# Keeping the whole TensorE stream in source order in a two-layer mixer kernel

## The chip, the cores and the metric

The kernel runs on one core of one Trainium2 chip. The metric is the device time of the launch in microseconds (us). Two runs of the kernel before gave 1919.79 and 1923.13 us, median 1921.46 us. A separate execution was profiled; its own time is 1923.45 us.

## The reference, cut to what matters

The program computes two layers of a hybrid backbone for 256 context tokens and 256 latent tokens of width 2048. In each layer the tokens are RMS-normed and modulated by a vector that comes out of `c_silu @ ada_w` (adaLN), go through one input projection `h @ w_in`, and are split into four head groups: bidirectional mLSTM, bidirectional retention, softmax attention with rotary positions, and bidirectional gated DeltaNet. Each group's output is multiplied by a SiLU gate, the groups are concatenated, go through `w_out`, are normed again and added to the stream. Layer 1 needs its latent half alone at the output. In short:

```
mod = silu(c) @ ada_w + ada_b
h   = rms_norm(x, pre_w) * (1 + sc) + sh
u   = h @ w_in                       # all four groups' q, k, v, gates
y   = [mlstm(u), retention(u), attention(u), gated_delta(u)]   # each * silu(z)
x   = x + gt * rms_norm(concat(y) @ w_out, post_w)
```

The mLSTM and the DeltaNet need gates: a log-sigmoid and a softplus of a few columns of `u`, then cumulative sums over tokens. The DeltaNet also needs a triangular solve per chunk and a state that is carried from chunk to chunk. All arithmetic is in float32; the large products split each operand into a rounded part and a remainder and add three products.

## The kernel before, in words

**The stream of large products.** A `Run` is one group of output columns of `w_in` or `w_out`. `emit` (L946) walks its contraction in steps of 128 rows (16 steps k), and each step adds three matmuls per output tile into a PSUM tile `acc` (L969), twelve in a step of four tiles. `Stream` (L899) loads a raw weight tile with a DMA on the SP queue (L915), rounds it on ScalarE (`whi`, L926) and takes the remainder on VectorE (`wlo`, L927); there are three `raw` tiles and four `whi` and `wlo` tiles, so splits run at most three steps ahead of the matmuls that use them. `acc` has four buffers. When a run's last two steps are done per output tile, `evac` takes the tile out of PSUM.

**The small work** is written as Python generators, one for each task: the gates (`gate_tiles`, L219), the mLSTM (L333), retention, attention (L499 on), the DeltaNet's solve, its doubling and its chunk recurrence (class `Delta`, `double`, `pair`), column sums, the transposes ahead of layer 1 (`h_half`, L1215) and those ahead of `w_out` (`transposed`, L1484 on). After each step k of the large stream, `emit` calls `pump`, which lets every live task emit its instructions up to its next `yield`. So the source order is: twelve large matmuls, a piece of each task, twelve large matmuls, and so on. `finish` runs a task to its end at one place, with no large matmuls between its pieces. Small PSUM results use a pool `mx` of three buffers.

**What sets the order on an engine.** The framework's scheduler orders each engine's instructions by its own reckoning of when inputs are ready; among ready instructions the one that comes first in the source goes first. [...] One place, the products with `ada_w` of layer 0 (`ada_products`, L1056 on, L1074), sits in a block `manual_schedule` for TensorE, in which the source order holds among the instructions of the block.

Names that the prediction uses: `gps` (L283 to L286) are the matmuls of the gates' cumulative sums, `g_lf` (L264) their last input; in layer 0 they are emitted after the first twelve matmuls of the run `m_k` that follows the gate columns' last evacuation. `a_pq` (L527) transposes softmax weights `a_p` (L520). `d_py` (L721) opens the DeltaNet's doubling, on tiles `d_T` that a DMA brings. `d_pu` (L838), `d_pS` (L851), `d_ks` (L826), `d_po` (L865, L867) are the steps of its recurrence, `d_W` (L804) the decayed scores that free the PSUM tile the second `d_pu` needs. `h_ps` (L1226) transposes the normed rows `yo` (L1186) for layer 1.

Of the kernel before, what the change touches and what calls it, by code (L numbers as in the profile page):

```python
# [70 lines left out]
def setup(ctx, tc, cst):  # L71
    E = Env()
    nc = tc.nc
    E.nc, E.tc = nc, tc
    E.clock = 0
    E.tasks, E.free, E.live = [], list(range(NSLOT)), {}
    E.cp = ctx.enter_context(tc.tile_pool(name="cp", bufs=1))
    E.ly = ctx.enter_context(tc.tile_pool(name="ly", bufs=1))
    E.bp = ctx.enter_context(tc.tile_pool(name="bp", bufs=1))
    E.tp = ctx.enter_context(tc.tile_pool(name="tp", bufs=5))  # L80
    E.sp = ctx.enter_context(tc.tile_pool(name="sp", bufs=1))
    E.wp = ctx.enter_context(tc.tile_pool(name="wp", bufs=4))
    E.hp = ctx.enter_context(tc.tile_pool(name="hp", bufs=8))
    E.acc = ctx.enter_context(tc.tile_pool(name="acc", bufs=4, space=PSUM))
    E.mx = ctx.enter_context(tc.tile_pool(name="mx", bufs=3, space=PSUM))
    E.dr = ctx.enter_context(tc.tile_pool(name="dr", bufs=1, space=DRAM))
    ct = E.ct = E.cp.tile([P, C_END], F32, name="ct")
    nc.scalar.dma_start(out=ct[:, :C_UP], in_=cst[:, :C_UP])
    E.ident = ct[:, C_ID:C_UP]
    E.up = ct[:, C_UP:C_LO]  # L90
    E.lo = ct[:, C_LO:C_COS]
    E.cos = ct[:, C_COS:C_SIN]
    E.sin = ct[:, C_SIN:C_DL]
    E.dl = ct[:, C_DL:C_END]
    E.ones = E.cp.tile([P, P], F32, name="ones")
    nc.gpsimd.memset(E.ones, 1.0)
    E.mhalf = E.cp.tile([P, 16], F32, name="mhalf")
    nc.gpsimd.memset(E.mhalf, -0.5)
    E.xd = E.dr.tile([2, 32 * 129 * P], F32, tag="xd", name="xd")
    return E  # L100
# [1542 lines left out]

@with_exitstack
def hybrid_dit(ctx: ExitStack, tc: tile.TileContext, I):
    nc = tc.nc
    E = setup(ctx, tc, I.cst)
    x_in = [I.ctx[0, 0:P], I.ctx[0, P:2 * P], I.x[0, 0:P], I.x[0, P:2 * P]]
# [172 lines left out]
```

## Time and profile before

| | |
|---|---|
| median of two runs | 1921.46 us |
| profiled execution, its time | 1923.45 us |
| profiled execution, its span | 1921.7 us |
| TensorE busy | 1848.4 us, 96% |
| VectorE busy | 1341.9 us, 70% |
| ScalarE busy | 813.1 us, 42% |
| mean granted TensorE clock | 0.992 |
| bytes moved | 344.84 MB, mean 179 GB/s |

The span is the time from the first to the last instruction; the execution's own time is 1.75 us longer. Busy time is the union of an engine's instruction records. PE is the matmul row of TensorE, PEld its weight loads, DVE is VectorE, ACT is ScalarE, SP the queue that issues DMAs. In the timeline a row may merge several instructions of a kind; the bracket at its end is the engine's idle time before it and what ended it.

### The profile page before, as it was taken

To read this page: it belongs to the slowest core of one execution; us is meant where nothing else is said; L and a number is where in the kernel's file an instruction comes from. 1 tells how busy PE (TensorE), PEld (TensorE's weight loads), DVE (VectorE), ACT (ScalarE), POOL (GpSimd) and SP (SyncE) were. 2 spreads that over 40 slices of the span, in tenths; PEclk is the share of its full clock that TensorE was granted. 3 is DMA by queue.
4 is the path that set the end of the run, shared out by engine and by line. 5 is a ranking of instruction groups with operands and counts; after the bars stand their busy time and mean duration, and the time that the engine had idled before them with its cause. 6 is when DMAs were issued, how large, how long until landed. Compare 5 with 4: busy or idle time off the path is not lost. (4 is left out here: it accounts for less than half of the span.)

```text
span 1921.7 us, 29531 instructions
## 1 busy us (share of the span) xinstructions
PE 1848.4 (96%) x10836; PEld 1527.6 (79%) x10836; DVE 1341.9 (70%) x2714; ACT 813.1 (42%) x1591; POOL 132.1 (7%) x162
## 2 busy tenths in 40 slices
PE   5999999999999999999999999999999999999997
PEld 3677887777878877788888868978988898888886
DVE  3455689999986896889743578347856476849765
ACT  5322333334342434434342456333435354446453
POOL 0000011121000100000000000000002010000000
PEclk8999999999999999999999999999999999999999
DMA  9887545666655649545423576535744255765464
GB/s 290 275 295 239 183 124 160 194 194 199 220 159 153 198 128 273 170 132 169 133 94 103 180 234 219 148 111 175 252 156 153 92 170 148 189 186 162 134 227 157
DMA packets 265294, 344.84 MB, mean 179 GB/s; under 512 B 48266, under 2 KB 142638, under 8 KB 265150
## 3 DMA queue, kind: packets, MB, share of 16 engines
q1 hardware_dynamic: 264416, 342.71, 57.5%
q8 instruction: 85, 1.39, 0.3%
q14 instruction: 59, 0.48, 0.1%
q10 hardware_dynamic: 734, 0.26, 0.1%
HBM read 321.26 MB, written 17.98 MB: 177 GB/s over the span
## 5 line engine op out<-in xcount | busy, mean ns | idle before, releaser
L926 ACT CAST whi<-raw 128x512 fp32r<-128x512 f32 (+2 forms) x736 | 426.6, 584 | 767.0 <-PE acc L969 667.3
L927 DVE TENSOR_TENSOR wlo<-raw,whi 128x512 fp32r<-128x512 f32 (+2 forms) x736 | 474.1, 649 | 346.7 <-ACT whi L926 338.2
L969 PE MATMUL acc<-h_hi,whi 128*128 128x512 f32 (+1 forms) x1088 | 410.5, 378 | 2.4 <-DVE yo L1555 2.4
L969 PE MATMUL acc<-h_hi,wlo 128*128 128x512 f32 (+1 forms) x1088 | 398.7, 368 | 2.9 <-DVE wlo L927 2.9
L969 PE MATMUL acc<-h_lo,whi 128*128 128x512 f32 (+1 forms) x1088 | 399.9, 368 | 0.0
L969 PE MATMUL acc<-whi,h_hi 128*128 128x512 f32 (+2 forms) x992 | 363.8, 367 | 8.2 <-DVE h_hi L1211 3.6
L969 PE MATMUL acc<-whi,h_lo 128*128 128x512 f32 (+2 forms) x992 | 349.5, 353 | 0.0
L969 PE MATMUL acc<-wlo,h_hi 128*128 128x512 f32 (+2 forms) x992 | 349.5, 353 | 0.0
L1110 DVE SCALAR_TENSOR_TENSOR ada_acc<-ada,c,ada_acc 128x512 f32<-128x512 f32 x448 | 322.1, 760 | 37.7 <-DMA ada<-in_ada_w_dram 32.3
L969 PEld LDWEIGHTS acc<-h_hi,whi 128*128 128x128 f32 x1088 | 206.0, 189 | 45.7 <-issue 7.4
L969 PEld LDWEIGHTS acc<-h_hi,wlo 128*128 128x128 f32 x1088 | 205.2, 189 | 38.8 <-DVE wlo L927 4.8
L969 PEld LDWEIGHTS acc<-h_lo,whi 128*128 128x128 f32 x1088 | 206.2, 190 | 31.9 <-issue 1.8
L969 PEld LDWEIGHTS acc<-whi,h_hi 128*128 128x128 f32 x992 | 188.5, 190 | 39.1 <-issue 6.7
L969 PEld LDWEIGHTS acc<-whi,h_lo 128*128 128x128 f32 x992 | 188.0, 190 | 25.1 <-issue 0.8
L969 PEld LDWEIGHTS acc<-wlo,h_hi 128*128 128x128 f32 x992 | 188.7, 190 | 21.8 <-issue 0.7
L969 PE MATMUL acc<-wlo,mT1h 128*128 128x512 f32 x96 | 38.9, 405 | 3.4 <-DVE wlo L927 3.4
L969 PE MATMUL acc<-whi,mT1h 128*128 128x512 f32 x96 | 38.6, 403 | 0.3 <-ACT mT1h L1513 0.3
L969 PE MATMUL acc<-whi,mT1l 128*128 128x512 f32 x96 | 38.7, 403 | 0.0
L969 PE MATMUL acc<-whi,mT0h 128*128 128x512 f32 x96 | 38.6, 402 | 0.0
L969 PE MATMUL acc<-wlo,mT2h 128*128 128x512 f32 x96 | 38.5, 401 | 0.0
L969 PE MATMUL acc<-wlo,mT0h 128*128 128x512 f32 x96 | 38.5, 401 | 0.0
L969 PE MATMUL acc<-whi,mT2l 128*128 128x512 f32 x96 | 38.1, 397 | 0.0
(369 smaller groups left out, 2338.9 us busy)
## 6 DMA issues: line engine op xcount, KB each, us to landing
raw<-in_w_in_dram SPq DMA_DIRECT2D x176, 512.0 KB, 3.7
ada<-in_ada_w_dram SPq DMA_DIRECT2D x128, 512.0 KB, 4.4
raw<-in_w_in_dram SPq DMA_DIRECT2D x160, 256.0 KB, 3.7
raw<-in_w_out_dram SPq DMA_DIRECT2D x80, 512.0 KB, 4.4
adq<-in_ada_w_dram SPq DMA_DIRECT2D x48, 512.0 KB, 5.6
xd<-zero SPq DMA_DIRECT2D x2, 2064.0 KB
ada<-in_ada_w_dram SPq DMA_DIRECT2D x16, 256.0 KB, 6.1
adq<-in_ada_w_dram SPq DMA_DIRECT2D x16, 256.0 KB, 5.2
```

What stands on the lines that cost most here:

```text
L926: nc.scalar.copy(hi, src)
L927: nc.vector.tensor_tensor(out=lo, in0=src, in1=hi.bitcast(F32), op=ALU.subtract)
L969: nc.tensor.matmul(dst, l, r, start=(i == 0 and j == 0), stop=(i == n - 1 and j == 2))
L1110: nc.vector.scalar_tensor_tensor(out=acc, in0=t, scalar=c, in1=acc, op0=ALU.mult, op1=ALU.add)
```

## The change

One line at the start of the kernel function puts all that follows in a `manual_schedule` block for TensorE alone. TensorE's instructions then stand in the order in which the source emits them, over the whole kernel. The other engines and the DMA queues are ordered by the scheduler as before. No instruction is added or removed.

```diff
 @with_exitstack
 def hybrid_dit(ctx: ExitStack, tc: tile.TileContext, I):
+    ctx.enter_context(tc.manual_schedule(engines={mybir.EngineType.PE}))
     nc = tc.nc
     E = setup(ctx, tc, I.cst)
```

## Rows read from the trace of the kernel before

**Rows 1.** The page: busy time of each engine, share of the span, instructions.
```profile
PE 1848.4 (96%) x10836; PEld 1527.6 (79%) x10836; DVE 1341.9 (70%) x2714; ACT 813.1 (42%) x1591; POOL 132.1 (7%) x162
```

**Rows 2.** TensorE's waits: total us, times, longest us.
```profile
PE acc L969 <- DVE wlo L927: 6.3, 5, 2.1
PE d_pu L838 <- DVE d_W L804: 3.8, 2, 2.0
```

**Rows 3.** Timeline of TensorE around 305 us and 357 us: start, duration, instruction.
```profile
305.64 0.94 PE L394 MATMUL m_po<-m_v,mp 128*128 128x129 f32 x6 [1.42 <-DVE mp L383]
306.33 0.48 PE L969 MATMUL acc<-h_hi,whi 128*128 128x512 f32 x1
...
357.08 0.39 PE L969 MATMUL acc<-whi,h_hi 128*128 128x512 f32 x1
357.30 0.39 PE L969 MATMUL acc<-wlo,h_hi 128*128 128x512 f32 x1
```

**Rows 4.** Timeline around layer 0's gates: ScalarE, VectorE, TensorE.
```profile
225.89 0.26 ACT L227 ACTIVATE ga_ax<-gt 128x64 f32<-128x64 f32 x1 [1.23 <-DVE gt L1281]
...
231.68 0.68 DVE L1307 TENSOR_TENSOR m_k<-m_k,acc 128x512 f32<-128x512 f32 x1
...
239.68 0.25 DVE L264 COPY g_lf<-ga_ax 128x16 f32<-128x16 f32 x2
...
239.91 0.40 PE L283 MATMUL gps<-g_lf,ct 128*128 128x16 f32 x2 [0.21 <-DVE g_lf L264]
```

**Rows 5.** The same three steps around layer 1's gates.
```profile
1247.18 0.26 ACT L227 ACTIVATE ga_ax<-gt 128x64 f32<-128x64 f32 x1
...
1257.54 0.25 DVE L264 COPY g_lf<-ga_ax 128x16 f32<-128x16 f32 x2
...
1257.76 0.40 PE L283 MATMUL gps<-g_lf,ct 128*128 128x16 f32 x2 [0.34 <-DVE g_lf L264]
```

**Rows 6.** Timeline: `a_p` on ScalarE, `d_pu` on TensorE, `yo` on VectorE.
```profile
727.72 0.78 ACT L520 ACTIVATE a_p<-a_ps,a_m,a_sc 128x512 f32<-128x512 f32 x1 [0.83 <-DVE a_m L518]
...
838.68 0.68 PE L838 MATMUL d_pu<-d_vA,d_T 128*128 128x128 f32 x4 [1.97 <-DVE d_W L804]
...
916.50 0.68 PE L838 MATMUL d_pu<-d_vA,d_T 128*128 128x128 f32 x4 [1.83 <-DVE d_W L804]
...
1186.19 1.42 DVE L1186 TENSOR_SCALAR yo<-yo,xss 128x1024 f32<-128x1024 f32 x2 [0.43 <-POOL xss L189]
```

**Rows 7.** Windows, large matmuls (L969) alone: stretch, length, busy (count), clock, DMA share, GB/s.
```profile
226.62:239.90 13.28, 13.08 (x58) 1.00 0.48 150
724.15:729.10 4.95, 4.95 (x23) 1.00 0.97 214
834.00:838.60 4.60, 2.71 (x11) 1.00 0.36 116
909.20:916.50 7.30, 5.47 (x23) 1.00 0.43 130
1180.00:1187.00 7.00, 6.09 (x49) 1.00 0.65 206
1248.70:1257.75 9.05, 8.72 (x39) 1.00 0.39 116
1803.00:1817.50 14.50, 6.87 (x17) 1.00 0.22 72
...
sum 45.76, PE 35.69; mean PE 2.38
```

**Rows 8.** TensorE's first large matmul; windows (last: L969 alone), clock third from the end.
```profile
39.68 0.60 PE L969 MATMUL acc<-whi,h_hi 128*128 128x272 f32 x1 [3.55 <-DVE h_hi L1211]
...
40.00:42.00 2.00, 2.00 (x9) 1.95 (x9) 1.71 (x6) 1.64 (x3) 0.00 (x0) 0.50 1.03 336
46.00:50.00 4.00, 4.00 (x32) 3.02 (x31) 1.93 (x9) 1.74 (x5) 0.00 (x0) 1.00 1.08 379
...
1823.70:1831.10 7.40, 6.88 (x16) 0.77 0.19 65
```

## The prediction

> **What bounds the kernel now.** The first view is the page's table of busy times: TensorE has work in 1848.4 of 1921.7 us, no other engine over 70% [rows 1]. What is left to win on TensorE is 73.3 us, and of these a good part lies before the large matmuls start (the first one begins at 39.68 us [rows 8]) and at the very end, some 40 us by my estimate from that. So a mere reordering of TensorE can hardly bring more than about 30 us, 1.6%.
>
> The second view is the list of TensorE's waits. They are short: the five waits on a weight remainder sum to 6.3 us, the two of `d_pu` on `d_W` to 3.8 [rows 2].
>
> The third view is TensorE's own timeline. Large matmuls of 512 columns start 0.22 to 0.23 us apart [rows 3]; that is the price of one matmul in what follows. And TensorE does not step over a matmul that waits: `m_po` waited 1.42 us for VectorE, and the large matmuls behind it started after it [rows 3]. What stands early in the list and is late in fact costs its whole wait.
>
> Then I laid the order in which the source emits matmuls beside that timeline. Most of the trace already follows the source. Where it departs, it nearly always does so in one direction: small matmuls of a task run later than the source puts them, and large matmuls fill the time. Rows 7 show how much filled it at each of the large places. These fillers move behind the small matmuls in the changed kernel.
>
> **The change, part by part.** Nothing is added, removed or resized. What is moved is the place of some small matmuls on TensorE, each ahead of the large ones that pass it now. While one waits, all large matmuls stand behind it; behind those stand ScalarE's `whi` and VectorE's `wlo` splits (their four buffers are freed by the matmuls) and, behind these, the SP queue's `raw` loads with three buffers. So in a wait those engines soon have only the chain that the small matmul waits for, which shortens it; that is my lower bound at each place. The upper bound is the filling work.
>
> *Gates, layer 0.* In the source, `gps` follows twelve matmuls after the gate columns are out; in the timeline that place is reached at 226.6 us. Its input chain starts on ScalarE at 225.89 and `g_lf` starts at 239.68; `gps` runs at 239.91 [rows 4], after 58 large matmuls, 13.1 us [rows 7]. In the chain's time VectorE also ran nine larger instructions (splits, evacuations), each taking about 0.6 us of the queue, one of 0.68 us shown [rows 4]. Without these 5.4 us the chain ends near 234.4: a wait of 7.8 us. I take 8.0 (7.8 to 13.1).
>
> *Gates, layer 1.* The same place is reached at 1248.7, the chain starts at 1247.18, `gps` runs at 1257.76 [rows 5], 39 matmuls filled 8.7 us [rows 7]. Three splits (1.8 us) lie in the chain: it ends near 1256, a wait of 7.2. I take 7.5 (7.2 to 8.7).
>
> *Attention at 724 us.* `a_pq` is reached at 724.15 and needs `a_p`, which ScalarE ends at 728.50 [rows 6], held up by gate work on VectorE that does not depend on TensorE's place. I take 4.3 (2.5 to 4.95, the filling work [rows 7]). `d_py`, 21 us later, counts among the small places.
>
> *The recurrence's second `d_pu`, layer 0.* Both wait 1.8 to 2.0 us for `d_W` after 11 and 23 matmuls have filled in [rows 6, 7], so the inputs are truly late: 2.7 and 5.1 (of 5.47), together 7.8 (5 to 8.2).
>
> *Context rows for layer 1.* `h_ps` is reached at 1180.0. Its four transposes need the second row block, scaled from 1186.19 to 1187.6 [rows 6], its first half by 1186.9. The filling is 6.1 us in 49 short matmuls [rows 7]. Two splits lie in VectorE's chain. I take 5.0 (3.5 to 6.1).
>
> *The recurrence in layer 1, second half.* `finish` emits it with no large matmuls between its steps. Now 17 of them slip in between 1803.0 and 1817.5 [rows 7]; 17 times 0.23 is 3.9. The steps' own latencies remain, so the 17 come later: 3.9 (2.5 to 3.9).
>
> *Small places.* Fifteen more stretches (the `ada_w` products waiting for their DMA, convolution before the first transposes in both layers, transposes ahead of `w_out`, sums and value transposes, later recurrence steps, `d_py`) hold 35.7 us of large matmuls [rows 7], of which about a third belongs ahead of the small matmul anyway or is counted twice where records overlap. I take 25 (12 to 35).
>
> The sum of these: 8.0 + 7.5 + 4.3 + 7.8 + 5.0 + 3.9 + 25 = 61.5 us.
>
> *The clock.* [...] Five of the new waits (two gates, `a_pq`, the second `d_pu` at 909, `h_ps`) are of 4 us or more. In mid-stream the row nearest to it is the stretch from 1823.7 to 1831.1, with a mean of 0.77 [rows 8]: 46% of 7.4 us, 3.4 us, at half rate, 1.7 us lost. Bounds for five waits are 0 and 15.6; by the mid-stream row, the nearer one, 5 times 1.7, I take 8.
>
> *Given back.* While TensorE stands, splits and evacuations catch up, and some of the waits on `wlo` (6.3 us [rows 2]) go; I take 6 off (0 to 10).
>
> In all 61.5 + 8 - 6 = 63.5 us. Against the profiled execution's 1923.45 us this gives 1987; the median is 2.0 us lower, so 1985 us, 3.3% slower. By the lower ends (40 for the places, no clock, 10 off) it is 1952; by the upper ends (80 for the places, 15.6 for the clock, nothing off) 2017.
>
> [...] TensorE's records overlap: a large matmul is 0.39 us long and the next starts 0.23 after it [rows 3], and weight loads are busy for 79% of the span [rows 1]. [...]
>
> **Rivals.** A program takes two runs within 0.2% here; a change under 2% (38 us, to 1960) I call no change.
>
> *The chains shrink: not slower.* Place: the gates, the recurrence and the small stretches. With TensorE standing, the other engines do the chain alone; if they end it in half of the filling time on the average, the waits sum to some 30 us, most are too short to lower the clock, and the time is 1951. It decides where the sum of all waits falls below 38 us. For it: 5.4 of the 13.8 us of layer 0's gate chain were other work, and the small places are mostly unproven. Against it: the places with proven lateness (the gates by chain length, `d_pu` by its own wait, `a_pq`) make over 25 us already. Chance 0.20.
>
> *Heavier.* The other engines' order, made anew around the waits, leaves the chains as long as now, every filler costs in full and every long wait lowers the clock: 45 + 36 + 15 = 96 us, 2017, and up to 2045 if late splits follow. For it: the trace's order of VectorE shows that unrelated work is put into these chains. Chance 0.15.
>
> *The order does not change.* The block around `ada_w` products did not keep them ahead of later matmuls from outside it; if the outer block did as little, the time stays 1921. The code gives no ground, since here every TensorE instruction is inside. Chance 0.02.
>
> *Faster.* [...] Chance 0.02.
>
> *The forecast*, 1962 to 2010: 0.61. The range that leaves out two in ten takes in the upper half of the not-slower case and the lower half of the heavier one: 1948 to 2022. Slower by over 2%: 0.61 + 0.15 = 0.76; within: 0.20 + 0.02 and the like, 0.22; faster: 0.02.
>
> **What would show it.** In the changed trace, `gps` follows twelve large matmuls after the last gate evacuation, with an idle time of about 8 us before it that `g_lf` ended, in both layers; `a_pq` has one of about 4 us; the second `d_pu` 3 to 5; `h_ps` near the boundary about 5. TensorE's waits sum to some 60 us more than now while the matmul count is the same. The granted clock falls to 0.5 behind the longest of them. I am wrong if the idle time before `gps` is under 4 us (the chain was cut by more than I see), if the waits are as foreseen but the end is not (then they were given back in the stream), or if the matmul order is as before.

## The result, and the profile after

The changed kernel takes 2013.04 us, median of two runs (2010.57 and 2015.51): 1.0467 of the kernel before, 95% interval 1.0404 to 1.053, some 92 us slower. Five later runs of the same kernel gave 2014.64 us, ratio 1.0472 [1.0446, 1.0498]; the experiments are compared with that. These five and the experiments ran on three chips, on which the kernel before has medians of 1929.84 us (`gps` later, four transposes, the smaller filling, the later half), 1924.25 (the five later runs, the first half, the mended source with and without source order) and 1926.03 (the rest). A ratio is always to the kernel before on the same chip, so where a difference of medians and one of ratios disagree, the ratio counts. The forecast was slower by 63.5 us, 1985 us, with 1962 to 2010 as its main case and 2022 as the upper end of its wider range. The direction and most of the places were right, the size was a third too small.

The page of the profiled run, busy times:

```profile
span 2013.8 us, 29536 instructions
...
PE 1877.3 (93%) x10836; PEld 1553.1 (77%) x10836; DVE 1349.0 (67%) x2714; ACT 817.1 (41%) x1591; POOL 132.4 (7%) x162
```

Set against [rows 1], TensorE has the same 10836 instructions. Time without a busy record on TensorE (span less busy) was 1921.7 - 1848.4 = 73.3 us and is 2013.8 - 1877.3 = 136.5 us: 63.2 us more waiting. Busy time itself grew by 28.9 us for the same matmuls: they ran slower. These two numbers make up the 92.1 us between the spans, and they are what the experiments have to explain.

TensorE's waits after (engine, what waited and for what: total us, times, longest):

```profile
PE gps L283 <- DVE g_lf L264: 16.4, 2, 8.5
PE h_ps L1226 <- ACT h_tmp L1228: 13.5, 16, 1.6
PE d_pu L838 <- DVE d_W L804: 12.1, 3, 6.8
PE h_ps L1226 <- DVE yo L1186: 7.2, 3, 2.8
...
PE d_kps L633 <- ACT d_k L566: 7.0, 4, 2.7
...
PE a_pq L527 <- ACT a_p L520: 5.6, 3, 4.3
...
PE acc L969 <- DVE wlo L927: 3.3, 3, 2.1
```

The head of the list is new. `gps` waits twice for `g_lf`; behind it stands `h_ps` on ScalarE's `h_tmp`, which the prediction had not seen; `d_pu` on `d_W` went from 3.8 [rows 2] to 12.1 us; and `acc` on `wlo` fell from 6.3 to 3.3. The same waits before, where [rows 2] do not have them:

```profile
PE a_pq L527 <- ACT a_p L520: 1.2, 1, 1.2
...
PE h_ps L1226 <- DVE yo L1186: 1.0, 3, 0.4
...
PE h_ps L1226 <- ACT h_tmp L1228: 0.7, 2, 0.5
```

The timeline around both gates (start, duration, instruction, in brackets the idle time before it and what ended it), to be read against [rows 4, 5]:

```profile
232.64 0.26 ACT L227 ACTIVATE ga_ax<-gt 128x64 f32<-128x64 f32 x1 [1.24 <-DVE gt L1281]
...
233.29 0.40 PE L969 MATMUL acc<-h_hi,wlo 128*128 128x512 f32 x1
...
236.74 0.63 DVE L927 TENSOR_TENSOR wlo<-raw,whi 128x512 fp32r<-128x512 f32 x1
...
241.97 0.25 DVE L264 COPY g_lf<-ga_ax 128x16 f32<-128x16 f32 x2
...
242.20 0.61 PE L283 MATMUL gps<-g_lf,ct 128*128 128x16 f32 x2 [8.51 <-DVE g_lf L264]
...
245.61 0.77 PE L969 MATMUL acc<-h_hi,whi 128*128 128x512 f32 x1
246.18 0.63 PE L969 MATMUL acc<-h_lo,whi 128*128 128x512 f32 x1
246.61 0.63 PE L969 MATMUL acc<-h_hi,wlo 128*128 128x512 f32 x1
...
248.69 0.40 PE L969 MATMUL acc<-h_lo,whi 128*128 128x512 f32 x1
248.93 0.40 PE L969 MATMUL acc<-h_hi,wlo 128*128 128x512 f32 x1
...
1317.43 0.39 PE L969 MATMUL acc<-h_hi,wlo 128*128 128x512 f32 x1
1325.76 0.61 PE L283 MATMUL gps<-g_lf,ct 128*128 128x16 f32 x2 [7.93 <-DVE g_lf L264]
```

`gps` starts 0.23 us after `g_lf`, as before. What changed is what precedes it: before, large matmuls up to its start; now nothing for 8.51 and 7.93 us. In layer 0 the chain from `ga_ax` on ScalarE to `g_lf` takes 9.33 us (232.64 to 241.97) where it took 13.79 (225.89 to 239.68 [rows 4]), with one split on VectorE left in it, the one shown. Then look at the starts behind it: 246.18 and 246.61 are 0.43 apart, 248.69 and 248.93 are 0.24 apart. The windows of TensorE after the waits (stretch, length, busy, then the granted clock third from the end) say why:

```profile
242.20:248.30 6.10, 5.85 (x20) 0.50 0.01 3
249.00:257.00 8.00, 8.00 (x46) 1.00 0.30 87
1325.80:1333.90 8.10, 7.97 (x25) 0.50 0.00 0
1336.00:1346.00 10.00, 10.00 (x51) 1.00 0.61 157
1617.50:1620.50 3.00, 3.00 (x8) 0.50 0.23 78
```

Behind each gate wait TensorE is busy and granted 0.50, then 1.00 again. The last row is the instructive one: the stretch at 1617 follows two short waits, of 0.85 and 1.21 us. The length of a wait alone does not tell, though: behind one of 2.70 us the clock stayed at 1.00 (timeline, then the window behind it):

```profile
1614.94 0.66 PE L633 MATMUL d_kps<-ct,d_k 128*128 128x128 f32 x4 [0.85 <-ACT d_k L566]
1616.81 0.66 PE L633 MATMUL d_kps<-ct,d_k 128*128 128x128 f32 x4 [1.21 <-ACT d_k L566]
...
1827.27 0.43 PE L198 MATMUL cs_ps<-d_qsq,ones 128*32 128x128 f32 x8 [2.70 <-ACT d_qsq L773]
...
1827.30:1834.00 6.70, 6.70 (x36) 1.00 0.39 98
```

The mean granted clock over the span is 0.972 against 0.992 before. The clock records of both runs hold two values alone, 0.50 and 1.00; with these two, that is (1 - 0.972) x 2 x 2013.8 = 113 us at half rate against 31 us. A part of this is idle time. The records show 17 stretches at 0.50 against 5; two against one of them lie in the prologue and one each behind the last matmul, so in the stream there are 14 against 3: eleven new ones, where I had counted five. The sums of the windows over all stretches in which TensorE works (length, TensorE busy), after and before:

```profile
sum 105.83, PE 78.06; mean PE 4.88
...
sum 20.47, PE 16.92; mean PE 4.23
```

TensorE is busy at half rate for 61.1 us more than before. At two levels, half of that, 30.6 us, is what the half rate cost, and it agrees with the 28.9 us by which busy time grew.

The waits near the boundary, in the timeline:

```profile
1237.91 0.30 PE L1226 MATMUL h_ps<-ct,yo 128*128 128x128 f32 x1 [2.03 <-DVE yo L1186]
1241.05 0.47 PE L1226 MATMUL h_ps<-ct,yo 128*128 128x128 f32 x1 [2.85 <-DVE yo L1186]
1242.24 0.69 PE L1226 MATMUL h_ps<-ct,yo 128*128 128x128 f32 x2 [0.71 <-ACT h_tmp L1228]
```

The first two rows are what I foresaw (the second row block comes late). The third is not: the second pair of transposes writes the tile that ScalarE is still reading for the first pair, and waits. That happens 16 times, 13.5 us in all; before it was twice, 0.7 us.

### The profile page after: what moved, and what is told of

It is laid out like the page before. It is cut to its first block, busy times and chain, and to the rows that moved or that the text cites. A ratio compares the mean times of both kernels' runs of the same rounds, so it can differ in the third digit from the quotient of the medians.

```text
span 2013.8 us, 29536 instructions
## 1 busy us (share of the span) xinstructions
PE 1877.3 (93%) x10836; PEld 1553.1 (77%) x10836; DVE 1349.0 (67%) x2714; ACT 817.1 (41%) x1591; POOL 132.4 (7%) x162
## 3 DMA queue, kind: packets, MB, share of 16 engines
q1 hardware_dynamic: 264416, 342.71, 55.5%
## 5 line engine op out<-in xcount | busy, mean ns | idle before, releaser
L969 PE MATMUL acc<-h_hi,whi 128*128 128x512 f32 (+1 forms) x1088 | 416.3, 383 | 0.2 <-DVE yo L1555 0.2
L969 PE MATMUL acc<-h_lo,whi 128*128 128x512 f32 (+1 forms) x1088 | 402.7, 370 | 0.0
L969 PE MATMUL acc<-h_hi,wlo 128*128 128x512 f32 (+1 forms) x1088 | 401.8, 369 | 0.0
L969 PE MATMUL acc<-whi,h_hi 128*128 128x512 f32 (+2 forms) x992 | 365.7, 369 | 12.6 <-ACT sg L1447 4.4
L969 PE MATMUL acc<-whi,h_lo 128*128 128x512 f32 (+2 forms) x992 | 351.1, 354 | 0.0
L969 PE MATMUL acc<-wlo,h_hi 128*128 128x512 f32 (+2 forms) x992 | 350.8, 354 | 0.0
L969 PEld LDWEIGHTS acc<-h_hi,whi 128*128 128x128 f32 x1088 | 208.7, 192 | 47.1 <-issue 9.4
L969 PEld LDWEIGHTS acc<-h_hi,wlo 128*128 128x128 f32 x1088 | 208.6, 192 | 35.1 <-DVE wlo L927 0.3
L969 PEld LDWEIGHTS acc<-h_lo,whi 128*128 128x128 f32 x1088 | 208.9, 192 | 31.9 <-issue 1.0
L969 PEld LDWEIGHTS acc<-whi,h_hi 128*128 128x128 f32 x992 | 189.7, 191 | 44.6 <-issue 7.8
L969 PEld LDWEIGHTS acc<-whi,h_lo 128*128 128x128 f32 x992 | 189.3, 191 | 25.8 <-DVE h_lo L1212 0.5
L969 PEld LDWEIGHTS acc<-wlo,h_hi 128*128 128x128 f32 x992 | 189.8, 191 | 22.6 <-issue 0.7
L969 PE MATMUL acc<-wlo,mT1h 128*128 128x512 f32 x96 | 38.0, 396 | 3.0 <-DVE wlo L927 3.0
L969 PE MATMUL acc<-whi,mT0h 128*128 128x512 f32 x96 | 39.1, 407 | 0.0
L969 PE MATMUL acc<-whi,mT2h 128*128 128x512 f32 x96 | 38.9, 405 | 0.0
L969 PE MATMUL acc<-wlo,mT2h 128*128 128x512 f32 x96 | 38.5, 402 | 0.2 <-DVE wlo L927 0.2
L969 PE MATMUL acc<-wlo,mT0h 128*128 128x512 f32 x96 | 38.4, 400 | 0.0
L969 PE MATMUL acc<-whi,mT2l 128*128 128x512 f32 x96 | 38.4, 400 | 0.0
L969 PE MATMUL acc<-whi,mT0l 128*128 128x512 f32 x96 | 38.2, 398 | 0.0
```

Of the source, the lines that this page charges most:

```text
L969: nc.tensor.matmul(dst, l, r, start=(i == 0 and j == 0), stop=(i == n - 1 and j == 2))
```

## The experiments

The theory: the 92 us are small matmuls that now wait where the source puts them, some 63 us, plus about 29 us in which TensorE runs at half rate behind these waits. Rival A: the clock costs nothing by itself. Rival B: not the place of the small matmuls but the other engines' new order, or a drift of the whole schedule, costs the time. The experiments are edits of the changed kernel where nothing else is said.

### gps later

```diff
-    yield
+    yield from pause(E, 12)      # in gate_tiles, ahead of gps
```

> The changed kernel with one edit: in both layers the source puts the seven gps matmuls about 12 us of the large stream later; nothing else moves by hand. Theory (the 92 us are waits of small matmuls that stand where the source puts them, plus half-rate clock behind the longer ones): both gps waits (16.4 us in all) and the half-rate stretches at 238 and 1320 us go, so 15 to 20 us of the 92 come back, about 1995 us. Rival A (the clock costs nothing by itself): 16.4 us of waits less some 10 us that the stream makes up behind them now, about 2006. Rival B (not the places of the small matmuls but the other engines' new order costs the time): the wait moves elsewhere, 2010 to 2016.

Measured: 1996.15 us, ratio 1.0365 [1.033, 1.04]; 18.5 us less than the changed kernel's 2014.64. One row of its timeline:

```profile
241.07 0.40 PE L283 MATMUL gps<-g_lf,ct 128*128 128x16 f32 x2 [1.76 <-DVE g_lf L264]
```

That 1.76 us is all that is left of the 16.4, and the matmuls of `gps` take 0.36 to 0.40 us again, not 0.58 to 0.61. (Behind it 3.4 us of TensorE's work are still at 0.50, where it was 6.2 us.) The time came down by more than the waits alone hold (16.4 - 1.8 = 14.6 us), by 18.5 us by the medians and 20.6 by the ratios, but the intervals are too wide to tell 14.6 from these. The profiled runs say it better: against a second profile of the changed kernel (span 2012.9, busy 1875.2 us) TensorE's idle time fell by 15.1 us and its busy time by 5.7, to 1869.5, with the same matmuls. That speaks against rival A, and against rival B: only the rest of the gates' task, from the seven matmuls of `gps` on, was moved in the source.

### Four transposes, then ScalarE

```diff
         for u in range(2):
             k = 4 * j + i + u
             for t in range(2):
                 nc.tensor.transpose(ps[:, u, ...], ...)
+        for u in range(2):
+            k = 4 * j + i + u
             nc.scalar.activation(tmp[:, u], ps[:, u], ...)
```

> The changed kernel with one edit: the transposes ahead of layer 1 put all four of a step into their PSUM tile before ScalarE reads any of it (before: two transposes, ScalarE, two transposes, ScalarE). Theory: the second pair waits for ScalarE's read of the same tile, 16 times about 0.84 us, 13.5 us, which my prediction did not see; with the edit this falls under 3 us and the time by 9 to 14 us, to about 2001. Rival A: the same, as these waits are short. Rival B: the waits are covered or move to the next tile, time 2010 to 2016.

Measured: 2003.25 us, ratio 1.0399 [1.037, 1.0429]; 11.4 us less by the medians, 14.0 by the ratios. No wait on `h_tmp` is left in the list, and TensorE's busy time is the 1875.2 us of the second profile of the changed kernel. The missed step is worth about the 13.5 us that its waits showed; the clock has no part in it.

### Filling the waits with useless work

```diff
+def fill(E, n):
+    ps = E.mx.tile([P, 512], F32, tag="ada", bufs=1, name="fill")
+    for _ in range(n):
+        E.nc.tensor.matmul(ps, E.ident, E.ct[:, 0:512], start=True, stop=True)
 ...
+    fill(E, 9)                              # ahead of gps
 ...
+                if i == 0 and d == 1 and t0 == 0:
+                    fill(E, 5 if pr == 0 else 7)   # ahead of the second d_pu
```

> The changed kernel with useless work added: 30 float32 matmuls of 128x512 into a PSUM tile that nobody reads, nine ahead of gps in each layer, five and seven ahead of the second d_pu of the two recurrences of layer 0; they are to keep TensorE busy while it waits, and take no wait away. Theory: the waits there are filled, the granted clock stays at 1.00 behind them (half-rate stretches at 238, 873, 952 and 1320 us go), and the time falls by 7 to 13 us, about 2003, though work was added. Rival A (clock costs nothing): no change, 2011 to 2016, or slower by what the filling overshoots.

Measured: 2009.49 us, ratio 1.0433 [1.04, 1.0465]; 5.2 us less by the medians, 7.5 by the ratios, at best the lower end of the 7 to 13 that the theory said, and by the intervals not apart from the changed kernel. The spans of the profiled runs differ by 7.1 us (2005.8 against 2012.9). The trace is clearer than the time:

```profile
231.20 7.88 PE L184 MATMUL fill<-ct 128*128 128x512 f32 x18
239.88 0.40 PE L290 MATMUL gps<-g_lf,ct 128*128 128x16 f32 x2 [0.80 <-DVE g_lf L270]
...
242.07 0.48 PE L978 MATMUL acc<-h_hi,whi 128*128 128x512 f32 x1
242.38 0.40 PE L978 MATMUL acc<-h_lo,whi 128*128 128x512 f32 x1
242.62 0.40 PE L978 MATMUL acc<-h_hi,wlo 128*128 128x512 f32 x1
```

`gps` is as late as ever (its chain is what it waits for), but the large matmuls behind it start 2.19 us after it and 0.24 apart, where they started 3.41 us after it and 0.43 apart in the changed kernel (242.20, 245.61). Since the time alone did not settle it, it was done again on a larger scale, with 57 such matmuls at ten places:

```diff
+            if t0 == 0 and h == 0 and s == 3:
+                fill(E, 4)                   # ahead of a late r_st
 ...
+        if t0 == 0 and (h, b) == (3, 3):
+            fill(E, 4)                       # ahead of the last a_pq
 ...
```

> The filling run again, with useless float32 matmuls at six more places of the changed kernel (57 in all: also ahead of a late retention block, of layer 0's first key transposes, of the last a_pq of layer 0, of its first d_py, of the first transposes of the context rows and of the last transposes of DeltaNet's output in layer 1). No wait is taken away. Theory (each half-rate stretch behind a wait costs about 2 us): half-rate time falls from 112 to under 60 us and the time by 11 to 18 us, 1997 to 2004. Rival A (the clock costs nothing by itself): 2012 to 2018.

Measured: 2000.48 us, ratio 1.04 [1.0369, 1.0432]; 14.2 us less than the changed kernel, with work added and no dependence taken away. Its page:

```profile
span 1999.2 us, 29760 instructions
...
PE 1904.2 (95%) x10950; PEld 1552.8 (78%) x10950; DVE 1346.9 (67%) x2714; ACT 816.3 (41%) x1591; POOL 134.5 (7%) x162
```

The mean granted clock is 0.990, that is 40 us at half rate. The 114 records of filling take 0.44 us each by the row above (7.88 us for 18), 50 us; busy time grew by 1904.2 - 1875.2 = 29 us against the profiled run of the five (1875.2 busy in 2012.9). So all other matmuls together took 21 us less, at the same shapes and in the same order. The clock's records agree: TensorE was busy at 0.50 for 74.7 us in that profile and for 28.3 us here, and half of the 46.4 us between is 23. The filling overshot the waits by 7 us (50 us against 42.7 us less idle time), and 21 - 7 is the 14 us measured. (Filling does not hold the clock at every place each time: in this profile 6.8 us of work behind layer 0's gate, from 239.8 on, are at 0.50.) Rival A is out.

### One half of the kernel at a time

The block opened only behind layer 0's first products, and the counterpart, closed there:

```diff
+    ctx.enter_context(tc.manual_schedule(engines={mybir.EngineType.PE}))
     layer_vectors(E, I, 1, V[1])
```

> The kernel before with the block opened later: the source order holds on TensorE only from behind layer 0's first products (about 350 us) to the end. Theory: the places add up, so the first part's share, about 15 us (6.7 in the prologue, 8.7 at layer 0's gates), is saved and the rest stays: about +76, 1997 us. Rival B (a drift of the whole order, in which early waits set the phase of the later ones): not additive, either nearly the whole 92 (over 2008) or clearly less than 65 (under 1986).

> The counterpart of the run in which the block opened late: source order on TensorE from the start to the end of layer 0's first products, the scheduler's from there on. Theory (places add up): the share that the other half lacked, 15 to 18 us, so 1.008 to 1.0095 of the kernel before. Rival B (early waits set the phase of what follows): more than 30 us, or nothing.

Measured: 1998.44 us, ratio 1.0378 [1.0347, 1.0408], for the later part; 1944.27 us, 1.0101 [1.0066, 1.0135], for the first (its runs lie far apart, 1933 to 1952; the median is a little above the 1.008 to 1.0095 that was expected, and the interval covers it). The shares 3.8% and 1.0% sum to 4.8%, against 4.7% for both. In the profiled runs it is 74.2 + 10.0 us by the spans, 84 of 92. Most of the 8 us between lie in the prologue: the 600th large matmul starts 6.8 us later than before in the changed kernel's profiled run and 0.9 us later in that of the first part alone, though both have the source order there (in the second profile of the changed kernel it is 4.0 us: the prologue differs from run to run). The costs add up place by place; a drift is not needed. What the first part costs is nearly all at layer 0's gates: between the 600th and the 900th large matmul the first part's lag grows by 11.3 us.

### Mending many places

Source order throughout, with pauses put into the source at seven places; and the same source without source order on TensorE:

```diff
+    yield from pause(E, 12)                      # gate_tiles, ahead of gps
 ...
+            yield                                # retention, after each block
 ...
+            yield from pause(E, 4)               # keys, layer 0
 ...
+        yield from pause(E, 9 if self.t0 == 0 else 5)   # double (was 5)
 ...
+            yield from pause(E, 8)               # pair, ahead of the recurrence, layer 0
 ...
+        yield from pause(E, 6)                   # behind the norms of latents and of context
```

with the four transposes of above.

> The changed kernel, TensorE still in source order throughout, but seven places of the source are mended by hand: gps 12 us later, four transposes before ScalarE reads them, the recurrences of layer 0 8 us later, DeltaNet key transposes of layer 0 4 us later, doubling of layer 0 4 us later, retention gives way after each block, and the transposes at the boundary wait 6 us longer behind the norms. Theory: the waits of these places sum to about 16 (gps) + 13 (h_tmp) + 12 (d_pu) + 5 (d_kps) + 4 (r_st) + 4 (d_py) + 5 (h_ps behind yo) = 59 us; with four fifths of it gone, and the half-rate time behind them, 45 to 60 us come back: 1952 to 1967. Rival B (the order of the other engines or a general drift costs the time): the waits reappear elsewhere, over 1980.

> The kernel before (TensorE ordered by the scheduler) with the same seven places of the source mended. Theory: the scheduler had moved these matmuls to about there already, so next to nothing changes: ratio to the kernel before 0.995 to 1.005. Rival (the mended source is better in itself, and e6 would gain for that reason): ratio under 0.99.

Measured: 1973.14 us, ratio 1.0261 [1.023, 1.0292]: 41.5 us came back, short of the 45 to 60. The same source under the scheduler: 1932.73 us, 1.0044 [1.0023, 1.0065]. So the mended source isn't better in itself, rather a little worse, and the gain belongs to the place of matmuls in TensorE's order. Where the theory overreached is in the waits of the mended kernel:

```profile
PE acc L972 <- DVE wlo L930: 9.2, 9, 1.9
...
PE cs_ps L198 <- ACT d_qsq L774: 7.7, 2, 5.4
```

A task that is delayed as a whole meets other work at its later steps: `cs_ps` waited 2.7 us in the changed kernel and 7.7 here, `wlo` 3.3 and 9.2. Rival B was right in this much: a wait can come back elsewhere if a chain is moved by hand.

### The buffer behind d_pu's wait

```diff
-            pq = PS(E, "d_qk")
+            pq = E.mx.tile([P, 512], F32, tag="ada", bufs=1, name="d_qk") if h == 0 else PS(E, "d_qk")
```

> The changed kernel with one edit: the first of the two score tiles ahead of the recurrence goes into a PSUM bank that lies idle after the prologue, so that the second d_pu finds a buffer of the pool free without waiting for VectorE's decayed scores d_W. Theory (the 11.3 us that the two second d_pu of layer 0 wait are for a PSUM buffer, not for data): these two waits fall under 1 us each; part of them comes back a step later, where d_po really needs d_W; in all 5 to 10 us less, 2004 to 2009. Rival (the wait is only moved): d_po or d_pS wait as long, 2011 to 2017.

Measured: 2008.07 us, ratio 1.0436 [1.0405, 1.0466]; 6.6 us less, inside the theory's range, though the interval still overlaps that of the changed kernel. `d_pu` no longer waits for `d_W`, but a part moved one step on:

```profile
PE d_pS L851 <- DVE d_W L804: 6.7, 2, 4.2
...
873.70 2.05 PE L851 MATMUL d_pS<-d_ue,d_kA 128*128 128x128 f32 x8 [2.47 <-DVE d_W L804]
```

Neither step reads `d_W` (the row shows what `d_pS` reads); both only lack a PSUM tile, which the instruction that writes `d_W` frees. So a pool of three tiles is part of the price of the fixed order: 12.1 us of waits on `d_W` became 6.7 with one tile more.

### A better mended version, and one for the kernel before

The mended version with the three pauses in the DeltaNet (keys, doubling, recurrence) taken out and the extra bank for `d_qk` put in:

> TensorE in source order throughout, with the places mended that need no later recurrence: gps 12 us later, four transposes before ScalarE reads them, retention gives way after each block, transposes at the boundary 6 us behind the norms, and the first score tile in the idle PSUM bank; DeltaNet's keys, doubling and recurrence start where the source has them. The earlier mended version lost some 15 us where its delayed recurrence ran out of large matmuls (its counterpart without source order lost as much there). Theory: 2014.6 less 18 (gps) 11 (h_tmp) 7 (d_pu) 4 (retention) 8 (boundary) gives about 1966, 1955 to 1972. Rival B (drift): waits reappear, over 1980.

Measured: 1966.31 us, ratio 1.022 [1.0188, 1.0252], 48.3 us less than the changed kernel: the parts, each measured by itself or read from its waits, add up. (The 15 us that this expectation gives for the delays was too much; by the ratio of the scheduler's counterpart, 0.4%, they cost about 8.) By the medians it is the fastest with the source order, and still slower than the kernel before: span less busy is 1966.0 - 1862.0 = 104 us, 31 us more than before, and the largest waits are at places that were not mended (`d_kps` 9.6 us, `d_pS` 6.8, `a_pq` 6.2, `d_py` 3.9).

And the kernel before with two edits that delay nothing, the four transposes and the extra bank:

> The kernel before, TensorE ordered by the scheduler, with two of the edits that delay nothing: four transposes before ScalarE reads them, and the first score tile in the idle PSUM bank. It tries for a version faster than both. Theory: the scheduler already fills these places, so at most the 3.8 us of d_pu's waits and their half-rate time come back: ratio 0.994 to 1.001.

Measured: 1921.23 us, ratio 0.9978 [0.9954, 1.0002]. The interval reaches 1: no gain is shown.

## Why the prediction was right in sign and short in size

**What held.** The mechanism did: no matmul starts on TensorE between 233.29 and 242.20, while `gps` waits its 8.51 us, so a small matmul that stands ahead of its inputs costs its lateness. Most of the large places came out near their terms. Gates: 8.51 and 7.93 us against 8.0 and 7.5. `a_pq` has one wait of 4.3, as said. The second `d_pu` of layer 0: 12.1 us less 1.0 (the third wait, in layer 1) less the 3.8 of before is 7.3 against 7.8. The estimates by the chain alone (7.8 and 7.2) were good to 0.8 us, so the reasoning that unrelated work on VectorE drops out of a chain while TensorE stands was right: in layer 0 one split of 0.63 us stayed in it, of nine larger instructions. The waits were not taken up by the rest of the stream: the whole 63.2 us of them stand in the span.

**The clock, the term that was too small.** "Five of the new waits (two gates, `a_pq`, the second `d_pu` at 909, `h_ps`) are of 4 us or more", and "5 times 1.7, I take 8". Measured: busy time grew by 28.9 us, of which filling alone recovered 21. Two things were wrong. The count: I let only waits of 4 us or more lower the clock, an estimate of mine that no row gave. Seven waits after the prologue are that long, and 0.50 stands behind each of them; seven more stretches at 0.50 stand behind waits of 1.2 to 3.6 us. The kernel before showed that already: the very stretch that I took the price from, at 1824 [rows 8], stands behind a wait of 2.02 us, in this row:

```profile
1822.97 0.30 PE L1507 MATMUL mT_ps<-ct,y_d 128*128 128x128 f32 x1 [2.02 <-DVE y_d L1468]
```

And the size: a short row in mid-stream gave 1.7 us. The 14 stretches in the stream hold 68.8 us of TensorE's work, so they cost 34.4 us, 2.5 each. At layer 0's gate seven `gps` matmuls took 3.41 us in place of 2.19, and six large ones came 0.43 apart for 0.23, another 1.2 us: 2.4 us; at layer 1's, the whole of 1325.8 to 1333.9 ran at 0.50. My upper bound of 15.6 was too low for the first reason: it held only five waits. The 3.1 us a wait in it was my estimate, and no run shows it as such; the 14 stretches cost from 1.5 to 4.1 us. Which of the short waits have 0.50 behind them stays open: 12 of the 19 between 1 and 3 us after the prologue have none within 1 us, and before the change one of the three stretches in the stream, at 1131 us, began 9 us behind the last wait of over 0.5 us.

**The boundary.** I took 5.0 us for `h_ps`. It was 20.7 us (13.5 on `h_tmp`, 7.2 on `yo`) against 1.7 before (0.7 and 1.0). I looked for late inputs and not at the source's own alternation: two transposes, ScalarE on the same tile, two transposes. As long as large matmuls slip in between, it costs next to nothing (0.7 us in all before); kept in order, it costs 0.84 us on the mean, sixteen times. The edit that undid it gave back 11.4 us by the medians.

**The small places** went the other way. Of the 63.2 us of new waiting, 15.9 are the gates (16.4 less the 0.55 of [rows 4, 5]), 4.4 `a_pq`, 7.3 `d_pu` and 19.0 `h_ps`; 16.6 are left for what I had at 25 (small places) + 3.9 (recurrence of layer 1) - 6 (given back), 22.9 us. I had taken two thirds of the filling work there; they cost less than that. So the sum of waits, 55.5 after what is given back, came near 63.2 partly by luck, by two errors of opposite sign. Of the 28.6 us between forecast (63.5) and spans (92.1) the clock makes 20.9 (28.9 less 8), the waits 7.7.

**Rivals.** "The chains shrink" is out by the size of the waits. "Heavier" was right on the clock ("every long wait lowers the clock": 0.50 stands behind all seven of 4 us or more) and wrong on its other half, since no gate chain cost its whole filling (8.51 us of 13.1, 7.93 of 8.7). That the order doesn't change is out by the timeline, and "Faster" by the time.

## What to carry to other kernels

Where a scheduler lets ready work pass a late matmul, the source order is not a harmless default: before fixing it, take each small step's lateness and ask what stands between two steps that share a tile. Price a wait on TensorE at its length plus the half rate behind it; here the second part was almost half of the first (28.9 to 63.2 us). Moving a late step back by hand helps where its chain is independent, and passes a part of the wait on where its successors share buffers.

## What the runs showed of the hardware that was not expected

A granted 0.50 stood behind short waits too: two of 0.85 and 1.21 us, one shortly after the other, were followed by it at 1617.5, while one of 2.70 us at 1824.57 was followed by 1.00. Useless matmuls made the kernel faster: 57 of them, 50 us of TensorE's time, shortened it by 14 us.
